# A Hymba block on one core: the MLP's first blocks by quarters of tokens, with their results kept in DRAM, and two orders between products

## The chip, the cores and the metric

The kernel runs on one core of a Trainium2 chip. The metric is the device time of one execution in microseconds (us). Three runs of the kernel before took 1572.6, 1574.49 and 1576.7 us; the median is 1574.49.

## The reference

One block of a streaming encoder, batch 1, 1024 tokens and 16 learned ones in front, width 1024, all float32. Cut to what matters here:

```python
h = concatenate([meta, x], axis=1)                      # 1040 tokens
h = h + token_mixer(rmsnorm(h, norm_mix_g), ...)        # ends with  mixed @ w_out
h = h + channel_mixer(rmsnorm(h, norm_ffn_g), ...)
return rmsnorm(h, norm_final_g)[:, N_META:]

def channel_mixer(u, w_up, w_gate, ffn_conv_w, w_down): # D_FF = 2816
    a = causal_dwconv(u @ w_up, ffn_conv_w)             # 3 taps along the tokens
    return (silu(a) * (u @ w_gate)) @ w_down
```

## The kernel before

Activations lie with features on the 128 partitions and tokens along the free axis. Every float32 matmul is made of three with a high and a low part of each operand (`mm3s`: high x high, low x high, high x low; lines L553, L554 and L555). ACT writes the high part of an operand (a cast, or a copy with a scale), DVE or POOL the low part (the difference).

Stages, in order of time: the mixer's projections and scans, head by head (to about 740 us); the output product with `w_out` (740 to 880); the second norm; the first block pair of the MLP; `xcomb`; the MLP's block pairs 1 to 10; the product with `w_down`; the last norm.

*Output product.* The class `Seven` makes a 2 x 2 block product from seven products instead of eight, in stages "1", "65", "73", "4" and "2"; `load`, `prep` (splits weights and sums of activations into parts) and `mms` (the matmuls) go step by step. Tokens are cut in two halves, A and B. Half B is complete after stage "73", so its norm runs beside stages "4" and "2"; half A is complete only at the end of stage "2", in two quarters of 256 tokens.

*Norm.* `rms` makes a column of sums of squares (`pcb`), takes root and reciprocal (`rcolb`), lets PE broadcast it along the partitions (`prb`), and ACT copies that to `Rb`. `scale_tasks` multiplies `resid` by `Rb` (L1026) and makes the high and low parts of the blocks `uh_g`/`ul_g` and `xh`/`xl` with the norm's gain (L967, L968).

*First block pair (pair 0).* `eight` makes it without sums of blocks: `pup` and `pga` are up and gate products, 24 matmuls each per output tile. `conv` applies the three taps on DVE (L1187, then two of L1189), silu on ACT (L1190) and the product with `Rb` (L1191, on DVE for pair 0, on POOL for the others); `gate` (L1223) multiplies with the gate product and writes the result to DRAM (`acts`), to be read by the last product.

*xcomb.* It makes the sums and differences of blocks that the products of seven need, for both quarters of a half (lines L964 to L993), eight calls of it.

*Pairs 1 to 10.* `seven(kind, i, ...)` with kind `up`, then `ga`: seven products into the PSUM banks x, y and z, in the order of `PROD`:

```python
PROD = (("x", 0, 0, 0), ("y", 0, 1, 1), ("x", 1, 0, 4), ("z", 1, 1, 3), ("x", 2, 0, 5), ("z", 2, 1, 2), ("x", 3, 0, 6))
```

Products 0 and 2 accumulate in x; ACT copies x out (`s2ga<-pga_x`, L1169) after product 2, and product 4 then goes on in the same bank. For `up` the tokens are in two chunks (258 and 256), for `ga` in one of 512. `need` loads and splits weights and runs its DVE steps (L261 to L266) and POOL steps (L243).

Which instruction comes first on an engine is decided when the program is built, by a list scheduler with planned times; code order and tile reuse bind it. `after(a, b)` binds one instruction to come behind another.

Of the kernel before, what the change touches and what calls it, by code (L numbers as in the profile page):

```python
# [17 lines left out]
P = 128  # L18
# [43 lines left out]
def body(ctx, tc, h_in, vecs, cst, mask_in, rot, w_v0, w_v, w_fm, w_out, w_up, w_gate, w_down, out):  # L62
# [234 lines left out]
    def rms(ss, t0, t1, nm, col, rb, ptags=("tr", "num"), eps=True):  # L297
# [14 lines left out]
        pr = rps("pr" + nm, ptags[1])  # L312
        for i, (o, w) in enumerate(subs):
            nc.tensor.matmul(pr[:, o:o + w], col[:w, i:i + 1].to_broadcast([w, P]), ident[:w, :w], start=True, stop=True)
        nc.scalar.copy(rb, pr[:, :n])
# [232 lines left out]
    def mm3s(pt, a, x, first, last):  # L548

        n = len(a)  # L550
        for k in range(n):
            (ah, al), (xh_, xl_) = a[k], x[k]
            nc.tensor.matmul(pt, ah, xh_, start=first and k == 0, stop=False, skip_group_check=True)  # L553
            nc.tensor.matmul(pt, ah, xl_, start=False, stop=False, skip_group_check=True)  # L554
            nc.tensor.matmul(pt, al, xh_, start=False, stop=last and k == n - 1, skip_group_check=True)  # L555
# [10 lines left out]
    class Seven:  # L566
# [3 lines left out]
        def __init__(self, nm, kn, wd, order, base, raw, rt, wlast, rlast, bank):  # L570
# [24 lines left out]

        def tsum(self, i, k):
# [3 lines left out]
        def prep(self, t):  # L600
# [5 lines left out]
            d = self.draws[t]  # L606
            act = self.act
            if st == self.order[-1]:
# [17 lines left out]
            else:  # L626
# [3 lines left out]
                self.ops[t] = [(half_of(w, 1), r7, "x"), (half_of(w, 0), r3, "y")]  # L630

# [73 lines left out]
    def wr(st, k, j):  # L705
        i = j + 2 * (k % 2) if st in ("65", "73") else k % 2 + 2 if st == "1" else k % 4
        if (st, k) == ("65", 0):
# [5 lines left out]
        return t[:, :HB], t[:, HB:2 * HB]  # L713

    def wbank(nm, b, j):
# [4 lines left out]
                 lambda k: tuple(wlate(x)[:, k * QT:(k + 1) * QT] for x in (0, 1)), wbank)  # L720
# [240 lines left out]
    def xput(i, k, j0, j1, src, g=None):  # L961
        hi, lo = (x[:, k, j0:j1] for x in xb(i))
        if g is None:
            nc.scalar.copy(hi, src)  # L964
            V.tensor_tensor(lo, src, hi.bitcast(F32), ALU.subtract)  # L965
        else:
            nc.scalar.activation(hi, src, AF.Copy, scale=g)  # L967
            V.scalar_tensor_tensor(lo, src, g, hi.bitcast(F32), ALU.mult, ALU.subtract)  # L968

    def xsingle(kb, t0, t1, half):  # L970
        g = vec[:, V_FFN + kb:V_FFN + kb + 1]
        i, o = ((kb // 4, TA), (2 if kb >= 4 else 6, TB))[half]
        xput(i, kb % 4, t0 - o, t1 - o, resid[:, kb, t0:t1], g)
# [4 lines left out]
    def xtile(nm, n):  # L978
        return fp2.tile([P, QT + 2], F32, tag="xc", name=nm, bufs=4)[:, :n]

    def xcomb(k, j0, j1):
# [5 lines left out]
        V.scalar_tensor_tensor(t3, B1, g1, u4, ALU.mult, ALU.subtract)  # L987
# [20 lines left out]
    def norm_tasks(t0, t1, mbs=range(KB), first=True):  # L1008
# [3 lines left out]
        def one(mb):  # L1012
            dst = ss if first and mb == mbs[0] else fp.tile([P, QT + 2], F32, tag="sqb", name=f"sqb{t0}_{mb}", bufs=2)[:, :n]
# [5 lines left out]
    def scale_tasks(t0, t1, tag):  # L1019
        def norm():  # L1020
            col = tmp.tile([P, 4], F32, tag="rcol", name=f"rcolb{t0}")
            rms(Rb[:, t0:t1], t0, t1, f"b{t0}", col, Rb[:, t0:t1], ptags=(tag, tag))

        def one(kb):
            x = resid[:, kb, t0:t1]
            V.tensor_tensor(x, x, Rb[:, t0:t1], ALU.mult)  # L1026
            xsingle(kb, t0, TA + XW if t1 == TB else t1, t0 >= TB)
# [15 lines left out]
    mixw.load(0)  # L1043
    mixw.load(2)
# [429 lines left out]
```

## Time and profile before

| | |
|---|---|
| median of three runs | 1574.49 us (1572.6 to 1576.7) |
| the profiled execution | 1575.96 us, span 1574.2 us |
| mean granted TensorE clock | 0.991 |
| busy: PE, DVE, ACT, POOL | 97%, 73%, 45%, 18% |
| one pair of the MLP's loop | 40.0 us |

The span is what the profiler recorded, from the first instruction to the last; the run's own time is 1.8 us longer. An engine's busy share is over the whole span. A row of the timeline gives start, duration, engine, line, operation and tiles, and in brackets how long the engine had been idle and what ended that. Lines are those of the kernel before.

### The profile page before, as it was taken

What the parts mean: (1) busy time and instruction counts of PE and PEld (TensorE: products, weight loads), DVE (VectorE), ACT (ScalarE), POOL (GpSimd) and SP (SyncE); (2) the same over time, 40 slices, a digit from 0 to 9 for tenths busy, and PEclk for the clock granted to TensorE, in tenths of its full rate; (3) what the DMA queues carried; (4) which work ended last, traced back from release to release, by engine and by line L of the source; (5) the groups of instructions that cost most, each with busy time, mean ns of one, the idle gap of its engine ahead of it and who ended that gap; (6) DMA issues with size and microseconds to landing.
All of it is one profiled execution on the core that took longest, in us unless ns stands there. A gap on an engine that the chain in (4) does not pass through costs nothing.

```text
span 1574.2 us, 25474 instructions
## 1 busy us (share of the span) xinstructions
PE 1524.2 (97%) x9701; PEld 1392.5 (88%) x9701; DVE 1146.2 (73%) x2342; ACT 714.1 (45%) x1468; POOL 277.3 (18%) x191
## 2 busy tenths in 40 slices
PE   7999999999999999999999899999999999999997
PEld 6999999999989999997888878888888888888876
DVE  8767768597858677679859787666676666777575
ACT  6574655545242535354347543333333334333363
POOL 0000000000000000000000005666666666000006
PEclk9999999999999999999999999999999999999999
DMA  6125445262625344245421111222222224832323
GB/s 211 41 69 170 153 119 181 81 217 88 213 80 176 115 147 144 88 130 197 175 90 58 48 38 72 79 81 80 75 81 81 81 81 150 331 111 90 103 65 108
DMA packets 86012, 184.83 MB, mean 117 GB/s; under 512 B 8249, under 2 KB 29441, under 8 KB 85889
## 3 DMA queue, kind: packets, MB, share of 16 engines
q1 hardware_dynamic: 85888, 183.20, 35.1%
q8 instruction: 76, 1.25, 0.3%
q14 instruction: 48, 0.39, 0.1%
HBM read 140.14 MB, written 43.03 MB: 116 GB/s over the span
## 4 chain that ended last, share of the span: by engine, by line
PE 79%; DVE 8%; DMA 7%; ACT 3%; issue 2%; POOL 1%; SPq 0%; DVEq 0%; ACTq 0%; POOLq 0%
PE pv L376 3%; PE pv L377 3%; PE pv L378 3%; PE po L388 3%; PE po L387 3%; PE po L386 3%; PE pga_x L553 2%; PE pup_x L553 2%; PE pup_x L555 2%; PE pup_x L554 2%; PE pga_x L555 2%; PE pga_x L554 2%; PE pdx L554 2%; PE pdx L555 2%; PE pdx L553 2%; PE pdy L553 2%
## 5 line engine op out<-in xcount | busy, mean ns | idle before, releaser
L1191 POOL TENSOR_TENSOR cv<-cv,Rb 128x512 f32<-128x512 f32 x40 | 62.9, 1573 | 993.4 <-ACT cv L1190 989.3
L376 PE MATMUL pv<-hi_v,uh 128*128 128x256 f32 (+1 forms) x512 | 146.6, 287 | 7.5 <-ACT hi_v L149 7.5
L378 PE MATMUL pv<-hi_v,ul 128*128 128x256 f32 (+1 forms) x512 | 145.1, 285 | 1.9 <-DVE ul L281 1.8
L377 PE MATMUL pv<-lo_v,uh 128*128 128x256 f32 (+1 forms) x512 | 145.6, 285 | 0.0
L386 PE MATMUL po<-uh,hi_o 128*128 128x386 f32 (+2 forms) x384 | 125.8, 328 | 0.0
L387 PE MATMUL po<-ul,hi_o 128*128 128x386 f32 (+2 forms) x384 | 123.8, 322 | 0.0
L388 PE MATMUL po<-uh,lo_o 128*128 128x386 f32 (+2 forms) x384 | 123.5, 322 | 0.0
L376 PEld LDWEIGHTS pv<-hi_v,uh 128*128 128x128 f32 x512 | 97.3, 190 | 10.1 <-ACT hi_v L149 7.5
L378 PEld LDWEIGHTS pv<-hi_v,ul 128*128 128x128 f32 x512 | 96.8, 190 | 2.4 <-DVE ul L281 2.3
L377 PEld LDWEIGHTS pv<-lo_v,uh 128*128 128x128 f32 x512 | 97.0, 189 | 1.0 <-DVE lo_v L150 0.9
L243 POOL TENSOR_TENSOR lo_ga<-fraw_ga,hi_ga 128x512 fp32r<-128x512 f32 (+1 forms) x50 | 87.1, 1749 | 40.4 <-ACT hi_ga L242 40.4
L243 POOL TENSOR_TENSOR lo_up<-raw_up,hi_up 128x512 fp32r<-128x512 f32 (+1 forms) x45 | 73.8, 1648 | 45.0 <-ACT hi_up L242 45.0
L242 ACT CAST hi_up<-raw_up 128x512 fp32r<-128x512 f32 (+1 forms) x52 | 36.4, 719 | 90.8 <-PE pga_z L554 46.9
L387 PEld LDWEIGHTS po<-ul,hi_o 128*128 128x128 f32 x384 | 72.9, 190 | 0.2
L386 PEld LDWEIGHTS po<-uh,hi_o 128*128 128x128 f32 x384 | 72.9, 190 | 0.1
L388 PEld LDWEIGHTS po<-uh,lo_o 128*128 128x128 f32 x384 | 72.7, 189 | 0.0
L554 PE MATMUL pup_x<-ul_g,hi_up 128*128 128x258 f32 (+1 forms) x240 | 67.1, 282 | 1.7 <-DVE ul_g L965 1.7
L242 ACT CAST hi_ga<-fraw_ga 128x512 fp32r<-128x512 f32 (+1 forms) x52 | 36.3, 717 | 70.1 <-PE pup_z L554 51.2
L553 PE MATMUL pup_x<-uh_g,hi_up 128*128 128x258 f32 (+1 forms) x240 | 67.1, 282 | 0.3 <-ACT s2up L1169 0.3
L555 PE MATMUL pup_x<-uh_g,lo_up 128*128 128x258 f32 (+1 forms) x240 | 66.1, 282 | 0.0
L386 PE MATMUL pq<-uh,hi_q 128*128 128x400 f32 (+2 forms) x192 | 63.1, 329 | 2.5 <-DVE vl L352 1.5
L386 PE MATMUL pk<-uh,hi_k 128*128 128x400 f32 (+2 forms) x192 | 62.4, 325 | 1.1 <-DVE kT L417 0.8
(701 smaller groups left out, 5166.4 us busy)
## 6 DMA issues: line engine op xcount, KB each, us to landing
wsd<-w_down_d SPq DMA_DIRECT2D x22, 512.0 KB, 4.2
wsd<-wsd SPq DMA_DIRECT2D x44, 256.0 KB, 2.1
raw_up<-w_up_d SPq DMA_DIRECT2D x22, 512.0 KB, 3.5
fraw_ga<-w_gate_d SPq DMA_DIRECT2D x22, 512.0 KB, 3.7
acts<-cv SPq DMA_DIRECT2D x44, 256.0 KB, 2.0
rd<-wsd SPq DMA_DIRECT2D x22, 512.0 KB, 3.4
wsw<-w_out_d SPq DMA_DIRECT2D x16, 512.0 KB, 4.2
raw_o<-w_fm_d SPq DMA_DIRECT2D x16, 512.0 KB, 3.5
```

The lines of the kernel that those rows point to most:

```text
L242: nc.scalar.copy(hi[:, o:o + n], x)
L243: (eng or nc.gpsimd).tensor_tensor(lo[:, o:o + n], x, hi[:, o:o + n].bitcast(F32), ALU.subtract)
L376: nc.tensor.matmul(pv[:L, :nv], a, hi[:, o:o + nv], start=kb == 0, stop=False)
L377: nc.tensor.matmul(pv[:L, :nv], a, lo[:, o:o + nv], start=False, stop=False)
L378: nc.tensor.matmul(pv[:L, :nv], b, hi[:, o:o + nv], start=False, stop=kb == KB - 1)
L386: nc.tensor.matmul(pt[:, :n], a, uh[kb][:, t0:t1], start=kb == 0, stop=False)
L387: nc.tensor.matmul(pt[:, :n], a, ul[kb][:, t0:t1], start=False, stop=False)
L388: nc.tensor.matmul(pt[:, :n], b, uh[kb][:, t0:t1], start=False, stop=kb == KB - 1)
L553: nc.tensor.matmul(pt, ah, xh_, start=first and k == 0, stop=False, skip_group_check=True)
L554: nc.tensor.matmul(pt, ah, xl_, start=False, stop=False, skip_group_check=True)
L555: nc.tensor.matmul(pt, al, xh_, start=False, stop=last and k == n - 1, skip_group_check=True)
L1191: (G if i else V).tensor_tensor(cv, cv, Rb[:, t0 + 2:t0 + XW], ALU.mult)
```

## The change

1. Pair 0's conv, silu, product with `Rb` and gate product leave the passage between norm and loop. `first_up` and `first_gate` copy the up and gate products out of PSUM and write them to DRAM (`kept`, eight writes). `gate_part(i)` for i = 1 to 4 calls `first_out`, which reads one (m, half) back and does `conv` and `gate` on it. The product with `Rb` is on POOL for all pairs.
2. The products of pair 0 for half A are cut by quarters of tokens: up (0 to 256, 256 to 514) and gate (2 to 256, 256 to 514), in the order up first quarter, gate first quarter, up second quarter, `xcomb` of the first quarter, gate second quarter, `xcomb` of the second.
3. Half B's norm is done in one piece of 514 tokens instead of 258 and 256.
4. Two orders: in `seven` the first product in z (n = 3) starts after product 2 has ended (`ends[2]`), and the first DVE operation of every `xcomb` but the first comes after the last scaled operand (`last["scaled"]`).
5. The output product's stage-4 weights are split during stages "65"/"73" into tiles of their own (`pre4`, `wfour`); weight loads go out four ahead of the reads (`pump`), and the tiles of stage 2's split weights are shared by halves.
6. The chunks of `up` are 256 and 258 wide; `xcomb`'s scratch tiles are shared in pairs with those that `first_out` reads into (`spare_out`).

The diff, cut to that:

```diff
+            if n == 3 and ci == 0:
+                after(m[0], ends[2])
+            ends[n] = m[1]
...
-        (G if i else V).tensor_tensor(cv, cv, Rb[:, t0 + 2:t0 + XW], ALU.mult)
+        nc.gpsimd.tensor_tensor(cv, cv, Rb[:, t0 + 2:t0 + XW], ALU.mult)
...
+    kept = {(kind, m, half): dram.tile([P, n], F32, name=f"kept_{kind}{m}{half}") for kind, n in (("up", XW), ("ga", HB)) for m in range(2) for half in range(2)}
+    UC = [(0, QT), (QT, XW)]
...
-            nc.scalar.copy(c0[m, half][:, slice(*chunks[ci])], pt)
-        eight("up", half, chunks, bank, done)
+            nc.scalar.copy(c0[m, half][:, slice(*UC[ci])], pt)
+            if ci:
+                nc.sync.dma_start(kept["up", m, half], c0[m, half][:, :XW])
+        eight("up", half, *UC[ci], lambda m: pp(f"pup0_{m}{half}{ci}", tags[m]), done)
...
+        def done(m, pt):
+            if j1 == XW:
+                x = ftile(f"g0_{m}{half}")
+                nc.scalar.copy(x[:, :HB], gbank[m, half])
+                nc.sync.dma_start(kept["ga", m, half], x[:, :HB])
+        eight("ga", half, j0, j1, bank, done)
...
-    def convs(half):
-        for m in range(2):
-            conv(0, m, half, c0[m, half])
-
-    first_up(1, lambda nm, m: pp(nm))
-    g = first_gate(1, lambda nm, m: pp(nm))
-    convs(1)
-    g()
-    first_up(0, lambda nm, m: fps(nm, "xy"[m]))
-    for k in range(4):
-        xcomb(k, 0, QT)
-    g = first_gate(0, lambda nm, m: fps(nm, "y"))
-    convs(0)
-    g()
-    for k in range(4):
-        xcomb(k, QT, XW)
-
-    UC = [(0, 258), (258, XW)]
+    def first_out(m, half):
+        c, g = (spare_out(f"{x}0b_{m}{half}") for x in "cg")
+        nc.sync.dma_start(c[:, :XW], kept["up", m, half])
+        nc.sync.dma_start(g[:, :HB], kept["ga", m, half])
+        conv(0, m, half, c)
+        gate(0, m, half, g[:, :HB])
+
+    for ci in range(2):
+        first_up(1, ci, ("pp", "pp"))
+    first_gate(1, 2, XW, ("pp", "pp"))
+    first_up(0, 0, ("pp", "sA"))
+    first_gate(0, 2, QT, ("sA", "num"))
+    first_up(0, 1, ("pp", "tr"))
+    for k in range(4):
+        xcomb(k, 0, QT)
+    first_gate(0, QT, XW, None)
+    for k in range(4):
+        xcomb(k, QT, XW)
...
         seven("ga", i, [(2, XW)], done)
+        if i < 5:
+            first_out((i - 1) % 2, (i - 1) // 2)
...
-    BQ, AQ = [(MB, MB + QT + 2), (MB + QT + 2, T)], [(MA, MA + QT), (MA + QT, MB)]
+    BQ, AQ = [(MB, T)], [(MA, MA + QT), (MA + QT, MB)]
...
+        if k or j0:
+            after(x, last["scaled"])
...
+            if mixw.steps[u][0] == "73" and u % 2 and u + 7 not in mixw.four:
+                mixw.pre4(u + 7)
```

ACT in the passage, where the second quarter of half A is normed, before (`sqb`: squares, `rcolb`: the root, `cv_11`: pair 0's conv result, `xu`, `xt`, `xv`: scratch of `xcomb`):

```order
L310 ACTIVATE rcolb_10438<-pcb_10439,epsc 128x2
L967 ACTIVATE uh_g<-xu_0_10836,vec 128x256
L964 CAST uh_g<-xv_0_10838 128x256
L986 ACTIVATE xu_0_10852<-resid,vec 128x256
L1190 ACT_TABLE_LOAD
L1190 ACTIVATE cv_11_10704<-cv_11_10704 128x512
L315 COPY Rb<-prb_10444 128x256
L964 CAST uh_g<-xt_0_10853 128x256
L967 ACTIVATE uh_g<-xu_0_10852,vec 128x256
L967 ACTIVATE uh_g<-resid,vec 128x258 x4
```

The same place in the changed kernel (`c`, `g`: copies of pair 0's products):

```order
L310 ACTIVATE rcolb_10389<-pcb_10390,epsc 128x2
L1270 COPY c_01_10514<-pup_011_10543 128x258
L1013 ACTIVATE xh_10205<-resid,vec 128x256
L1010 CAST uh_g<-xv_0_10824 128x256
L1013 ACTIVATE uh_g<-xu_0_10823,vec 128x256
L1270 COPY c_11_10541<-pup_111_10570 128x258
L1284 COPY g_01_10634<-pga_01_10609 128x512
L319 COPY Rb<-prb_10395 128x256
L1013 ACTIVATE uh_g<-resid,vec 128x258 x4
```

Between the root and the copy of `Rb` the table load and the silu are gone, and copies of products stand there.

PE at the same place, before: `prb` and the products that come next.

```order
L555 MATMUL pup_100_10741<-xh_10248,lo_up_1_10243 128x256
L304 MATMUL pcb_10439<-cs,Rb 128x1 x2
L314 MATMUL prb_10444<-cs,rcolb_10438 128x128 x2
L553 MATMUL pup_101_10794<-uh_g,hi_up_1_10242 128x258
L553 MATMUL pga_000_10884<-uh_g,hi_ga_0_10526 128x512
```

Now (`pup_100`, 24 matmuls, and the first quarter of `pga_00`, 24 matmuls, follow `prb`; `pup_101`, the first that reads the second quarter, stands 49 rows behind it, and `pcb` 50 rows ahead):

```order
L560 MATMUL pga_01_10609<-xh_9830,lo_ga_0_10486 128x512
L316 MATMUL prb_10395<-cs,rcolb_10389 128x128 x2
L558 MATMUL pup_100_10692<-uh_g,hi_up_1_10199 128x256
L559 MATMUL pup_100_10692<-ul_g,hi_up_1_10199 128x256
L560 MATMUL pup_100_10692<-uh_g,lo_up_1_10200 128x256
```

Before, `pcb` and `prb` followed the same up product, and the second quarter was read right behind them.

ACT in the loop around `s2ga`, in pair 2, before:

```order
L1190 ACTIVATE cv_01_11598<-cv_01_11598 128x512
L1169 COPY s0ga_11671<-pga_x_11658 128x512
L1190 ACTIVATE cv_10_11645<-cv_10_11645 128x512
L242 CAST hi_ga_3_11689<-fraw_ga_1_11380 128x512
L1169 COPY s2ga_11705<-pga_x_11658 128x512
L242 CAST hi_up_0_11722<-raw_up_0_11604 128x1024
```

and now, with the silu of the deferred piece (`cv_10_11779`):

```order
L1247 ACTIVATE cv_01_11589<-cv_01_11589 128x512
L1226 COPY s0ga_11662<-pga_x_11649 128x512
L242 CAST hi_ga_3_11680<-fraw_ga_1_11359 128x512
L1247 ACTIVATE cv_10_11636<-cv_10_11636 128x512
L1247 ACTIVATE cv_10_11779<-cv_10_11779 128x512
L1226 COPY s2ga_11696<-pga_x_11649 128x512
```

The cast of `hi_ga_3` has moved ahead of the silu of `cv_10`, and the deferred piece's silu stands between that and `s2ga`. DVE there, now (`c0b`: read back from DRAM):

```order
L261 TENSOR_TENSOR s_6_11751<-raw_up_1_11597 128x512
L1244 TENSOR_SCALAR cv_10_11636<-c_10_11633,vec 128x512
L1244 TENSOR_SCALAR cv_10_11779<-c0b_11775,vec 128x512
L262 TENSOR_TENSOR raw_up_1_11597<-raw_up_1_11597,raw_up_0_11595 128x512
L1246 SCALAR_TENSOR_TENSOR cv_10_11636<-c_10_11633,vec,cv_10_11636 128x512
L1246 SCALAR_TENSOR_TENSOR cv_10_11779<-c0b_11775,vec,cv_10_11779 128x512
L1246 SCALAR_TENSOR_TENSOR cv_10_11636<-c_10_11633,vec,cv_10_11636 128x512
L1246 SCALAR_TENSOR_TENSOR cv_10_11779<-c0b_11775,vec,cv_10_11779 128x512
```

Every second operation is the deferred piece's; before, `cv_10`'s three stood there alone. On PE, the gate product of a pair was y, ten matmuls of z's first product, x's product 2 (twelve), two of z and x's product 4; it is y, twelve of x, twelve of z, and product 4.

More of the change, by code (lines that the diff above doesn't have):

```diff
@@ L1012, in one @@
         def one(mb):
[L1013 removed]
+            dst = ss if first and mb == mbs[0] else (ftile(f"sqb{t0}_{mb}") if n > HB else fp.tile([P, QT], F32, tag="sqb", name=f"sqb{t0}_{mb}", bufs=2))[:, :n]
             nc.scalar.activation(dst, resid[:, mb, t0:t1], AF.Square)
@@ L1079, in body @@
             break
-        for u in range(t, t + 5):
-            mixw.load(u)
+        if t == 0:
+            mixw.pump()
         if st == "65" and k == 1:
@@ L1118, in body @@
     for k in range(KW):
-        for u in range(T2 + k, T2 + k + 5):
-            mixw.load(u)
         mixw.prep(T2 + k + 1)
@@ L1150, in seven @@
         banks = {}
+        ends = {}
         j00 = chunks[0][0]
```

124 lines of the change are left out of this document (83 added, 41 removed).

## The prediction

> **What bounds the kernel now.** I read the page first, then the table of stretches, then the waits of PE, and last the timeline of the stretches where PE waits. Ahead of everything stands one fact of the page: PE is the engine that counts.
>
> ```profile
> span 1574.2 us, 25474 instructions
> PE 1524.2 (97%) x9701; PEld 1392.5 (88%) x9701; DVE 1146.2 (73%) x2342; ACT 714.1 (45%) x1468; POOL 277.3 (18%) x191
> ```
>
> Only 50 us of the span are idle on PE, and the change keeps the number of products, so it can win only PE's idle time and time at a low clock. It touches two places: the passage from the output product to the MLP (850 to 951 us) and the MLP's loop. The stretches (span, then PE, PEld, DVE, ACT, POOL, clock, DMA share, GB/s) show where these lose:
>
> ```profile
> 900.00:905.00 5.00, 1.02 (x6) 0.66 (x4) 3.79 (x11) 4.06 (x9) 0.00 (x0) 0.59 0.00 0
> 905.00:910.00 5.00, 3.14 (x11) 2.51 (x11) 5.00 (x15) 2.12 (x7) 0.00 (x0) 0.50 0.00 0
> 940.00:945.00 5.00, 2.62 (x18) 2.02 (x16) 5.00 (x13) 2.39 (x6) 0.00 (x0) 1.00 0.42 129
> 1000.00:1040.00 40.00, 39.80 (x254) 35.74 (x253) 27.50 (x34) 14.03 (x27) 25.87 (x17) 1.00 0.26 80
> ```
>
> The loop has little to give: PE is busy 39.80 us of 40. The passage has two holes, around 900 and 941. Of PE's waits the longest of the passage (850 to 980) and the only one of the loop (965 to 1345) are (us in total, times, longest):
>
> ```profile
> PE pup L553 <- ACT uh_g L967: 4.0, 1, 4.0
> ```
>
> ```profile
> PE pga_x L553 <- ACT s2ga L1169: 2.6, 10, 0.8
> ```
>
> **Part 1: the three stalls of the passage, as they are priced now.** The timeline of PE:
>
> ```profile
> 857.14 0.40 PE L553 MATMUL pup<-xh,hi_up 128*128 128x256 f32 x2
> 858.66 0.38 PE L554 MATMUL pup<-xl,hi_up 128*128 128x256 f32 x1 [1.12 <-DVE xl L968]
> ...
> 899.64 0.71 PE L314 MATMUL prb<-cs,rcolb 128*128 128x128 f32 x4 [1.10 <-DVE rcolb L311]
> 904.33 0.58 PE L553 MATMUL pup<-uh_g,hi_up 128*128 128x258 f32 x1 [3.98 <-ACT uh_g L967]
> 907.20 0.58 PE L554 MATMUL pup<-ul_g,hi_up 128*128 128x258 f32 x1 [1.86 <-DVE ul_g L968]
> ...
> 911.20 0.29 PE L554 MATMUL pup<-ul_g,hi_up 128*128 128x258 f32 x1
> ...
> 943.58 0.39 PE L554 MATMUL pup_x<-ul_g,hi_up 128*128 128x258 f32 x1 [1.70 <-DVE ul_g L965]
> ...
> 945.37 0.58 PE L553 MATMUL pup_z<-uh_g,hi_up 128*128 128x258 f32 x1 [1.05 <-DVE cv L1223]
> ...
> 948.74 0.28 PE L553 MATMUL pup_z<-uh_g,hi_up 128*128 128x256 f32 x1
> ```
>
> - Stall 0 (half B's low parts, `xl`): the two matmuls from 857.14 take 0.40 us where one alone takes 0.28 (948.74), so matmuls of this width follow each other every 0.12 us and the next could start at 857.38; it starts at 858.66: 1.3 us.
> - Stall 1 (second quarter of half A): idle 1.10 + 3.98 + 1.86 = 6.9 us. From there matmuls run at half clock until 911.20 (the stretch 905 to 910 shows 0.50): from 904.33, 6.9 us less the 1.86 idle, 5.0 us at half speed, 2.5 lost. Together 9.4 us.
> - Stall 2 (the sums `xcomb` for the first block pair of seven products): idle 1.70 + 1.05 us, and half clock from 945.37 to 948.74, of which half, 1.7, is lost. Together 4.5 us.
>
> Why stall 1 is there is in the rows of ACT and DVE at that moment:
>
> ```profile
> 899.95 1.28 ACT L1190 ACT_TABLE_LOAD   x1
> 901.25 0.63 ACT L1190 ACTIVATE cv<-cv 128x512 f32<-128x512 f32 x1
> 901.78 0.36 ACT L315 COPY Rb<-prb 128x256 f32<-128x256 f32 x1
> ...
> 903.37 0.51 ACT L967 ACTIVATE uh_g<-xu,vec 128x256 fp32r<-128x256 f32 x1 [0.93 <-DVE xu L990]
> ...
> 901.91 0.69 DVE L1191 TENSOR_TENSOR cv<-cv,Rb 128x512 f32<-128x512 f32 x1 [1.21 <-ACT cv L1190]
> ...
> 903.25 2.77 DVE L1026 TENSOR_TENSOR resid<-resid,Rb 128x256 f32<-128x256 f32 x8
> ...
> 906.27 0.48 DVE L968 SCALAR_TENSOR_TENSOR ul_g<-xu,vec,uh_g 128x256 fp32r<-128x256 f32 x1
> ```
>
> The scale row `Rb`, for which `prb` was just made, is copied by ACT only behind a table load and a silu of block pair 0; DVE then stands on a `cv` operation and scales the quarter only at 903.25.
>
> **What the change does to them.** In the new order no conv, silu, Rb or gate operation of pair 0 lies in the passage. What leaves DVE there is in the view of one tile, `cv`, from 870 to 946:
>
> ```profile
> L1189 DVE SCALAR_TENSOR_TENSOR cv<-c,vec,cv x8: 744/746/749, 877.9 to 938.6; 128x512 f32<-128x512 f32 x8
> L1187 DVE TENSOR_SCALAR cv<-c,vec x4: 479/480/482, 877.1 to 931.6; 128x512 f32<-128x512 f32 x4
> L1191 DVE TENSOR_TENSOR cv<-cv,Rb x4: 679/688/693, 881.4 to 942.5; 128x512 f32<-128x512 f32 x4
> L1223 DVE TENSOR_TENSOR cv<-pga,cv x4: 678/684/691, 896.7 to 945.2; 128x512 f32<-128x512 f32 x4
> ```
>
> 8 x 0.746 + 4 x (0.480 + 0.688 + 0.684) = 13.4 us; as back-to-back operations overlap by some 0.08 us, about 11.7 of DVE's time.
> - Stall 0: half B's norm in one 514-wide piece puts its first products behind the whole of stage 2 (some 6 us later on PE), where its `xl` has been written. Gain 1.3 us. Bounds: 0 if the 514-wide square sums make the norm end just as much later, 1.3 at the best.
> - Stall 1: the copy of `Rb` loses the silu in front of it, `prb` goes ahead of a whole up-product of 24 matmuls, and 24 matmuls of the gate product's first half (254 wide) are put between that and the first one that needs the second quarter. That is 48 x 0.12 = 5.8 us of cover, against a chain from `prb` (Rb copy 0.36, eight scalings 2.77, then a scale by ACT like the one at 903.37, 0.51, and a low part by DVE like the one at 906.27, 0.48) of 4.1 us. All 9.4 us go; bounds 4.7 (the DVE chain is again held up by something in front) and 9.4.
> - Stall 2: PE reaches the sums about 1.3 + 9.4 = 10.7 us earlier. DVE has 11.7 us less, but not all of it lies ahead of the sum that PE waits for: of the four gate operations two lie at 944.63 or later, and in the new order DVE waits some 2 us for a cast by ACT. I walked the new DVE order from the second quarter's scaling on (50 operations of the sums at about 0.39 us, 6.7 us of others between them) and come out 0 to 4 us behind PE. I take 2 us of idle time and, since 1.70 + 1.05 us of idle cost a halved clock, another 1.5: 3.5 left of 4.5, a gain of 1.0. Bounds: loss 1.5, gain 4.5.
> - The split gate product has 96 matmuls of half the width for 48 of 512: two of 0.12 us against one of some 0.235 (two starts below, 1011.56 and 1011.79, lie 0.23 apart), so 0.2 us more.
> - The stage-4 operands split ahead, the halved stage-2 tiles and earlier loads (`pump`) lie in stretches where PE doesn't wait: nothing, bounds -0.5 and +1.
>
> The Trainium skill ("TensorE: Matmul & The Clock Gate", the Part 1 on the HAM clock gate) says that the clock is halved after an idle window of about 3.4 us and restored after about 3.4 us of work. The 3.37 us at half clock from 945.37 agree with the second number; the first doesn't, since the idle pieces there were 1.70 and 1.05 us. By the rule my residual stall of 2 us would cost only itself, and the sum would be 1.5 us better.
>
> Passage: -1.3 - 9.4 - 1.0 + 0.2 = -11.5 us.
>
> **Part 2: the loop.** The timeline of one iteration, PE first, then ACT, DVE and POOL of the iteration after:
>
> ```profile
> 1010.62 0.40 PE L555 MATMUL pga_z<-uh_g,lo_ga 128*128 128x512 f32 x1
> 1011.22 0.50 PE L553 MATMUL pga_x<-uh_g,hi_ga 128*128 128x512 f32 x1 [0.20 <-ACT s2ga L1169]
> 1011.56 0.39 PE L554 MATMUL pga_x<-ul_g,hi_ga 128*128 128x512 f32 x1
> 1011.79 0.40 PE L555 MATMUL pga_x<-uh_g,lo_ga 128*128 128x512 f32 x1
> ...
> 1049.20 0.63 ACT L1190 ACTIVATE cv<-cv 128x512 f32<-128x512 f32 x1 [5.18 <-DVE cv L1189]
> 1049.74 0.60 ACT L242 CAST hi_ga<-fraw_ga 128x512 fp32r<-128x512 f32 x1
> 1050.60 0.59 ACT L1169 COPY s2ga<-pga_x 128x512 f32<-128x512 f32 x1 [0.26 <-PE pga_x L555]
> ...
> 1042.80 1.78 DVE L261 TENSOR_TENSOR s<-raw_up 128x512 f32<-128x512 f32 x1
> 1044.50 1.52 DVE L1187 TENSOR_SCALAR cv<-c,vec 128x512 f32<-128x512 f32 x1
> 1045.94 1.78 DVE L262 TENSOR_TENSOR raw_up<-raw_up,raw_up 128x512 f32<-128x512 f32 x1
> ...
> 1045.70 1.47 POOL L1191 TENSOR_TENSOR cv<-cv,Rb 128x512 f32<-128x512 f32 x1
> 1049.91 1.73 POOL L1191 TENSOR_TENSOR cv<-cv,Rb 128x512 f32<-128x512 f32 x1 [2.74 <-ACT cv L1190]
> ```
>
> Bank x is wanted again when ACT has copied it (`s2ga`). PE's gap is 1011.22 - 1010.62 - 0.23 = 0.37 us, and the restart, 0.34 to the next instead of 0.23, makes it 0.48. With `after`, the x product ends 10 x 0.23 = 2.3 us sooner and twelve z matmuls (2.8 us) cover the copy. But the copy stays behind silu and cast on ACT: it could start at 1049.74 + 0.60 = 1050.34 instead of 1050.60. So 0.3 us are won per iteration, at most 0.48: six iterations (5 to 10) give -1.8.
>
> In iterations 1 to 4 a deferred piece of pair 0 is worked in: DVE gets a TENSOR_SCALAR and two SCALAR_TENSOR_TENSOR between those of `cv_10`, ACT a silu ahead of `s2ga`, POOL one more product with Rb, DVE a gate product. DVE is full from 1042.80 on. The added TENSOR_SCALAR meets POOL at work until 1045.70 + 1.47 = 1047.17, so it costs about 1.5 like the one at 1044.50; `L262` then runs after POOL and is 1.1 shorter (0.69 like L1191's above, for 1.78). The first added SCALAR_TENSOR_TENSOR costs 0.66 (0.746 less the overlap), so `cv_10` is ready about 1.5 - 1.1 + 0.66 = 1.0 later. Behind it come two silus of 0.55 and the copy (0.59); the cast goes ahead. From 1049.20 + 1.0, the copy ends near 1051.9; PE would go on at 1050.8 (0.37 before the copy's present end, 1050.60 + 0.59): a stall of 1.0 instead of 0.48, so +0.5 each, +2.0. Bounds per iteration: -0.5 and +2.5.
>
> Loop: -1.8 + 2.0 = +0.2 us (bounds -4.7 and +10).
>
> **Sum.** -11.5 + 0.2 = -11.3 us. The profiled execution took 1575.96 us (span 1574.2), so 1564.7 by its own time. It stands 1.5 us above the median of the runs, 1574.49; against that the sum gives 1563.2, the forecast. The range of the terms: -9.4 - 1.3 - 4.5 - 4.7 with the split's 0.2 gives 1554.8; the poor ends together (stall 1 at 4.7, stall 2 at +1.5, loop +5 at half its bound) 1576.
>
> **The rivals.**
> - *More is won*: stall 2 vanishes, too, and the loop wins 0.4 each time: -9.4 - 1.3 - 4.5 + 0.2 - 4 = -19 us, 1555.5. For it: DVE loses 11.7 us of work and ACT two table loads of 1.28. Against: DVE is at 5.00 of 5 around 941. Chance 0.15.
> - *DVE becomes the bound of the passage*: the second quarter or the sums come only half as much earlier, since the products with Rb were never what filled DVE: stall 1 gives 4.7, stall 2 loses 1.5: -1.3 - 4.7 + 1.5 + 0.2 = -4.3, with the loop 1570.4. Chance 0.13.
> - *Slower: the deferred conv runs into POOL.* Where POOL is busy, DVE's TENSOR_TENSOR takes 1.78 us (1042.80) and its TENSOR_SCALAR 1.52 (1044.50). If POOL, with one more product of 1.5 us per iteration, works on beyond 1047.17, the three added DVE operations cost 1.5 + 1.7 + 1.7 (the 1.78 less the overlap), `cv_10`'s own two 1.0 more each, and the added silu 0.55: 7.5 us on `s2ga`, 7 on PE, 28 in four iterations: -11.5 - 1.8 + 28 = +14.7, 1589. It decides from 13.3 / 4 = 3.3 us of added wait per iteration on. Against it: POOL sits idle for 2.74 us before 1049.91 and is busy only 25.87 us of 40. Chance 0.09. The Trainium skill ("GPSIMD Engine Reference", Specifications) states that POOL's SBUF interface is shared with VectorE's instructions that read two SBUF inputs or run in a 2-port mode, which speaks against moving this work next to POOL; the rows at 1042.80 and 1044.50 agree.
> - *Nothing moves*: half B's norm in one piece holds up the first products by as much as the rest wins: 1574. Chance 0.06.
>
> **How the numbers follow.** My forecast, 1558 to 1568, has 0.57. About 0.3% (4.7 us) is what a measurement of this kernel can tell from no change, so faster means below 1569.8. Forecast and first rival are faster, of the second some half: 0.79. Same: the other half and most of the last, 0.11. Slower: 0.10. The range takes in the second rival and most of the first: 1553 to 1572.
>
> **Signs.** Right: PE's waits for `uh_g`, `ul_g` in `pup` are gone, and the clock is 1.00 between 885 and 905; the first pair's `pup_x` begins some 11 us earlier; ACT's copy of `Rb` follows no table load; what is left of idle time is in front of pair 1's products, 1 to 3 us; `pga_x` waits for `s2ga` near 0.5 to 1 us in four iterations and 0.2 or less in six. Wrong: a new wait of PE in stage 2 or at the first `pup`, DVE operations of 1.5 us between `cv_10` and `s2ga` right up to the silu, or iterations 1 to 4 over 41 us.

## The result and the profile after

| | before | changed |
|---|---|---|
| median of twelve runs each | 1574.41 us (1571.8 to 1579.1) | 1576.64 us (1572.2 to 1581.8) |
| ratio | | 1.0012, 95% interval 0.9998 to 1.0026 |
| the profiled execution (span) | 1575.96 us (1574.2) | 1575.30 us (1573.2) |

No change that can be measured, where 11 us less were forecast; 1576.64 lies above the forecast's range of 1553 to 1572. The page of the changed kernel, its first line and the line of engines:

```profile
span 1573.2 us, 25559 instructions
PE 1528.0 (97%) x9749; PEld 1398.2 (89%) x9749; DVE 1157.6 (74%) x2318; ACT 711.4 (45%) x1457; POOL 283.1 (18%) x195
```

The two profiled executions already differ ahead of the changed passage. One product of the output product that stands alike in both starts 3.20 us earlier in the second. Over all kernels of this document its start varies from 739.3 to 745.2 us, so this says nothing of the change, and everything below is counted from it (before, then changed; timeline of PE):

```profile
743.66 0.47 PE L553 MATMUL pwy<-wtq,hi_w 128*128 128x512 f32 x1 [0.79 <-DVE mm L854]
```

```profile
740.46 0.47 PE L558 MATMUL pwy<-wtq,hi_w 128*128 128x512 f32 x1 [0.79 <-DVE mm L900]
```

The views of the tiles `pup_x` and `pga_y` (ns min/median/max, first and last start) give the first product of pair 1 and its first gate product in y, before and then changed:

```profile
L553 PE MATMUL pup_x<-uh_g,hi_up x240: 276/282/387, 934.1 to 1314.0; 128*128 128x258 f32 x70, 128*128 128x256 f32 x50
L553 PE MATMUL pga_y<-xh,hi_ga x40: 391/394/397, 962.4 to 1324.9; 128*128 128x512 f32 x40
```

```profile
L558 PE MATMUL pup_x<-uh_g,hi_up x240: 275/282/582, 919.9 to 1312.5; 128*128 128x256 f32 x69, 128*128 128x258 f32 x51
...
L558 PE MATMUL pga_y<-xh,hi_ga x40: 391/394/397, 949.9 to 1323.5; 128*128 128x512 f32 x40
```

So the execution splits into four pieces (us; the third ends with the loop's last matmul of `pga_x`):

| piece | before | changed | difference | forecast |
|---|---|---|---|---|
| mark to first `pup_x` (stalls 0 and 1, the split) | 190.4 | 179.5 | -10.9 | -10.5 |
| first `pup_x` to first `pga_y` (stall 2) | 28.4 | 30.0 | +1.6 | -1.0 |
| first `pga_y` to the loop's end | 378.7 | 389.7 | +11.0 | +0.2 |
| from there to the end | 233.1 | 233.6 | +0.5 | 0 |

They sum to +2.2, like the difference of the medians; such close agreement is luck, as single executions of one kernel spread over 7 to 10 us. Ahead of the first `pup_x` the gain came as forecast, and the loop took it back. PE's waits from 700 to 990 in the changed kernel, and below them those of the loop (965 to 1345):

```profile
PE pga_x L558 <- ACT s2ga L1226: 2.7, 1, 2.7
PE pup_x L559 <- DVE ul_g L1011: 1.0, 1, 1.0
PE pup_z L559 <- DVE ul_g L1014: 0.8, 1, 0.8
...
PE pup_x L558 <- ACT uh_g L1010: 0.6, 1, 0.6
```

```profile
PE pga_x L558 <- ACT s2ga L1226: 6.7, 4, 2.0
```

The waits of `pup` for `uh_g`, `ul_g` and `xl` (4.0, 1.9 and 1.1) are gone. What was 0.2 us in each pair is 2.7 and three times 2.0. The stretches show it by place: full clock where stall 1 was, a stall 2 as large as ever at 930, and four iterations of 42 to 44 us before they come down to 39.7:

```profile
900.00:905.00 5.00, 5.00 (x42) 4.91 (x42) 2.97 (x5) 2.10 (x2) 0.00 (x0) 1.00 0.12 10
...
930.00:935.00 5.00, 2.50 (x9) 1.45 (x7) 4.40 (x9) 3.51 (x7) 1.27 (x1) 0.89 0.00 0
935.00:940.00 5.00, 5.00 (x22) 4.61 (x22) 2.61 (x7) 2.00 (x6) 0.00 (x0) 0.50 0.37 105
```

```profile
949.93:994.10 44.17, 41.44 (x254) 37.03 (x252) 34.37 (x38) 14.98 (x28) 28.32 (x19) 0.96 0.27 90
994.10:1037.45 43.35, 41.40 (x253) 36.91 (x252) 33.54 (x38) 14.98 (x28) 27.49 (x18) 0.96 0.26 92
1037.45:1079.35 41.90, 39.91 (x254) 35.85 (x253) 33.19 (x38) 14.98 (x28) 27.61 (x18) 1.00 0.29 95
1079.35:1122.75 43.40, 41.45 (x253) 36.96 (x252) 33.56 (x38) 14.99 (x28) 27.52 (x18) 0.96 0.23 79
1122.75:1162.45 39.70, 39.70 (x253) 35.80 (x252) 27.56 (x34) 14.35 (x27) 26.09 (x17) 1.00 0.23 80
```

No engine but PE is anywhere near full in these iterations: DVE 34.4 of 44, POOL 28. It is one chain at one place. The timeline there, PE, then DVE, POOL and ACT:

```profile
958.09 0.39 PE L560 MATMUL pga_z<-uh_g,lo_ga 128*128 128x512 f32 x1
961.20 0.80 PE L558 MATMUL pga_x<-uh_g,hi_ga 128*128 128x512 f32 x1 [2.73 <-ACT s2ga L1226]
...
952.73 1.51 DVE L1244 TENSOR_SCALAR cv<-c,vec 128x512 f32<-128x512 f32 x1
954.16 1.51 DVE L1244 TENSOR_SCALAR cv<-c0b,vec 128x512 f32<-128x512 f32 x1
955.59 1.78 DVE L262 TENSOR_TENSOR raw_up<-raw_up,raw_up 128x512 f32<-128x512 f32 x1
957.28 0.74 DVE L1246 SCALAR_TENSOR_TENSOR cv<-c,vec,cv 128x512 f32<-128x512 f32 x1
957.95 0.74 DVE L1246 SCALAR_TENSOR_TENSOR cv<-c0b,vec,cv 128x512 f32<-128x512 f32 x1
958.61 0.74 DVE L1246 SCALAR_TENSOR_TENSOR cv<-c,vec,cv 128x512 f32<-128x512 f32 x1
...
955.33 1.48 POOL L243 TENSOR_TENSOR lo_ga<-fraw_ga,hi_ga 128x512 fp32r<-128x512 f32 x1
...
959.38 1.29 ACT L1247 ACTIVATE cv<-cv 128x512 f32<-128x512 f32 x2 [6.02 <-DVE cv L1246]
960.58 0.57 ACT L1226 COPY s2ga<-pga_x 128x512 f32<-128x512 f32 x1
```

The order is the one shown ahead of the prediction. The surprise is `L262`: 1.78 us, not 0.69, while POOL works on `lo_ga` beside it (955.33 to 956.81). That is the low part of `hi_ga_3`, whose cast moved ahead of the silus on ACT; e8 below tests that it is the cause.

### The profile page after: what moved, and what is told of

It is laid out like the page before. It is cut to its first block, busy times and chain, and to the rows that moved or that the text cites. A ratio compares the mean times of both kernels' runs of the same rounds, so it can differ in the third digit from the quotient of the medians.

```text
span 1573.2 us, 25559 instructions
## 1 busy us (share of the span) xinstructions
PE 1528.0 (97%) x9749; PEld 1398.2 (89%) x9749; DVE 1157.6 (74%) x2318; ACT 711.4 (45%) x1457; POOL 283.1 (18%) x195
## 4 chain that ended last, share of the span: by engine, by line
PE 79%; DVE 8%; DMA 7%; ACT 3%; issue 2%; POOL 1%; SPq 0%; DVEq 0%; ACTq 0%; POOLq 0%
PE pv L380 3%; PE pv L381 3%; PE pv L382 3%; PE pga_x L558 2%; PE pup_x L559 2%; PE po L391 2%; PE po L392 2%; PE po L390 2%; PE pup_x L558 2%; PE pup_x L560 2%; PE pga_x L559 2%; PE pga_x L560 2%; PE pdx L559 2%; PE pdx L560 2%; PE pdx L558 2%
## 5 line engine op out<-in xcount | busy, mean ns | idle before, releaser
L1248 POOL TENSOR_TENSOR cv<-cv,Rb 128x512 f32<-128x512 f32 x44 | 67.6, 1541 | 980.3 <-ACT cv L1247 967.9
L559 PE MATMUL pup_x<-ul_g,hi_up 128*128 128x256 f32 (+1 forms) x240 | 68.2, 286 | 1.0 <-DVE ul_g L1011 1.0
L558 PE MATMUL pup_x<-uh_g,hi_up 128*128 128x256 f32 (+1 forms) x240 | 68.0, 285 | 0.6 <-ACT uh_g L1010 0.6
L560 PE MATMUL pup_x<-uh_g,lo_up 128*128 128x256 f32 (+1 forms) x240 | 66.7, 284 | 0.0
```

What stands on the lines that cost most here:

```text
L558: m.append(nc.tensor.matmul(pt, ah, xh_, start=first and k == 0, stop=False, skip_group_check=True))
L560: m.append(nc.tensor.matmul(pt, al, xh_, start=False, stop=last and k == n - 1, skip_group_check=True))
L1248: nc.gpsimd.tensor_tensor(cv, cv, Rb[:, t0 + 2:t0 + XW], ALU.mult)
```

## The experiments

All are compared with the kernel before, run on the same chip; the rows come from several chips, so rows are compared by their ratios. The pieces are those of the table above, each read from one execution's timeline (mark to first `pup_x`; mark to first `pga_y`; the loop). The changed kernel, e1, e2 and e8 have the same instructions up to `pga_y` but for small swaps, and differ there by up to 1.6 us: a smaller difference in the first two pieces shows nothing.

| kernel | median, us | ratio (95%) | to `pup_x` | to `pga_y` | loop |
|---|---|---|---|---|---|
| before | | 1 | 190.4 | 218.8 | 378.7 |
| changed | 1576.64 | 1.0012 (0.9998 to 1.0026) | 179.5 | 209.5 | 389.7 |
| e1, silu behind | 1571.11 | 0.9965 (0.9952 to 0.9977) | 179.5 | 209.5 | 384.0 |
| e2, conv and silu behind | 1564.13 | 0.9924 (0.9911 to 0.9938) | 178.0 | 207.9 | 377.6 |
| e3, no deferred work | 1563.69 | 0.9922 (0.9909 to 0.9935) | 181.1 | 211.3 | 376.4 |
| e8, cast behind (one run) | 1571.95 | | 177.9 | 207.9 | 383.8 |
| e4, z order alone | 1576.38 | 0.9997 (0.9984 to 1.0010) | 191.8 | 220.8 | 375.6 |
| e5, conv back in the passage | 1568.74 | 0.9958 (0.9943 to 0.9974) | 179.0 | 212.6 | 377.4 |
| e9, e2 with whole gate product | 1563.93 | 0.9924 (0.9903 to 0.9946) | 178.5 | 205.7 | 378.4 |
| e12, e5 with whole gate product | 1571.27 | 0.9973 (0.9958 to 0.9988) | 181.2 | 214.6 | 377.1 |
| e15, e2 with norm in two pieces | 1565.98 | 0.9937 (0.9916 to 0.9958) | 180.2 | 209.2 | 378.2 |
| e16, e12 with norm in two pieces | 1572.09 | 0.9977 (0.9959 to 0.9996) | 182.9 | 216.7 | 376.9 |
| e17, order of sums alone | 1571.37 | 0.9982 (0.9967 to 0.9997) | 188.3 | 216.7 | 378.6 |
| e7, e2, pair 1's conv and silu behind | 1566.55 | 0.9941 (0.9923 to 0.9959) | 179.5 | 204.1 | 383.2 |
| e10, e2, pair 1's silu behind | 1560.73 | 0.9901 (0.9886 to 0.9916) | 178.0 | 205.4 | 378.5 |
| e11, e2, table load early | 1566.79 | 0.9938 (0.9922 to 0.9953) | 181.0 | 209.7 | 378.6 |

### Where the loop lost it: e1, e2, e3, e8

In `conv`, cut to the orders (`x` is its first DVE operation, `y` its silu); e2 has both, e1 the second alone:

```diff
+        if i == 0:
+            after(x, last["conv"])      # DVE: behind cv_10's last operation
...
+        if i == 0:
+            after(y, last["s2"])        # ACT: behind the copy s2ga
```

> The changed kernel, with one more order on ACT: the silu of the deferred piece of pair 0 (iterations 1 to 4) stands behind the copy s2ga, not ahead of it. DVE, POOL and PE keep their order. Theory A (the stall before x's product 4 in iterations 1 to 4 is DVE's chain: the added operations between those of cv_10 make cv_10 late by 2 to 3 us, the added silu only adds 0.6): PE still waits for s2ga in all four iterations, 0.6 us less each, 2.1 us in the first and 1.4 in the others; first to last gate product of the loop 3 to 7 us shorter, the upper end if no half clock follows. Rival B (the added silu is what holds the copy): no wait left in the four iterations and the loop 14 us shorter, about 1562 us.

> The changed kernel, with two more orders in iterations 1 to 4: the deferred piece's first DVE operation stands behind the last conv operation of cv_10, and its silu behind the copy s2ga. The same work is done. Theory A (order on DVE and ACT is the whole of the loss): cv_10's silu comes at the same place of the iteration as in iterations 5 to 10, PE's wait for s2ga falls from 1.95 to 2.73 us to under 0.3 in all four, periods 39.7 instead of 41.9 to 44.2, 14 us less, about 1562 us. Rival C (DVE, POOL or the queue of loads have no room for the deferred work in these iterations, wherever it stands): PE waits elsewhere in them, periods stay over 41, less than 6 us gained.

With the silu behind (e1), the waits are 2.13, 1.29, 1.36 and 1.29 us, 0.6 to 0.7 less each, and the loop is 5.7 us shorter: theory A's size, and rival B falls. In three iterations the clock stays up, too (41.16 to 41.28 us). With the conv's DVE operations behind as well (e2), PE waits for `s2ga` twice in the whole loop, in the first pair (0.68) and the last (0.77); e2's waits of PE from 885 to 1345:

```profile
PE pga_x L558 <- ACT s2ga L1226: 1.4, 2, 0.8
PE pup_x L559 <- DVE ul_g L1011: 1.0, 1, 1.0
PE pup_z L559 <- DVE ul_g L1014: 0.8, 1, 0.8
PE pup_x L558 <- ACT uh_g L1010: 0.5, 1, 0.5
```

The same work is done in the same iterations, and the loop is 12.1 us shorter. Rival C falls: DVE, POOL and the queue have the room.

```diff
-        if i < 5:
-            first_out((i - 1) % 2, (i - 1) // 2)
-                nc.sync.dma_start(kept["ga", m, half], x[:, :HB])
+                nc.sync.dma_start(acts[m, half], x[:, :HB])
```

> The changed kernel without the deferred work: pair 0's conv, silu, product with Rb and gate product are left out, and the gate product alone is written to DRAM in their place. This prices the deferred work in the loop. Theory A: periods 39.7 in all iterations, passage as in the changed kernel, 14 us less than it, within 1 us of the run with both orders. Rival C: clearly below that run. Rival D (the loss is not in the deferred work, but in the clock after the long stall of the passage): periods of 42 and more stay.

e3 has the time of e2 (0.9922 and 0.9924) and periods of 39.7 but for a first one of 40.3. In the two profiles the loop is 1.2 us shorter without the deferred work; once in order, that work is free to within what these runs can tell, and rival D falls.

```diff
+        # fstep, the last piece of the gate weights, pairs 1 to 4
+        after(last["cast"], last["silu"])    # ACT: cast of hi_ga_3 behind cv_10's silu
```

> The changed kernel with one order on ACT in pairs 1 to 4: the cast of the gate weights' last piece (hi_ga_3) stands behind the silu of cv_10 again, as in the kernel before; deferred work where it is in the changed kernel. It asks why DVE's L262 still took 1.78 us where the forecast had 0.69. If it is POOL's low part of that weight, which the earlier cast lets run beside L262: L262 0.7 to 0.8 us in pairs 1 to 4, the silu of cv_10 1.1 us earlier against y's first product, PE's waits for s2ga 1.95 less 1.1, plus the cast's 0.5 which now stands between, so 1.4. If POOL's product with Rb alone does it: L262 stays over 1.5 and the waits grow by 0.5.

The timeline of e8 (a single run) at the same place, DVE, POOL, ACT:

```profile
956.83 1.51 DVE L1247 TENSOR_SCALAR cv<-c0b,vec 128x512 f32<-128x512 f32 x1
958.26 0.68 DVE L262 TENSOR_TENSOR raw_up<-raw_up,raw_up 128x512 f32<-128x512 f32 x1
...
962.90 1.73 POOL L243 TENSOR_TENSOR lo_ga<-fraw_ga,hi_ga 128x512 fp32r<-128x512 f32 x1
...
960.96 0.63 ACT L1250 ACTIVATE cv<-cv 128x512 f32<-128x512 f32 x1 [6.06 <-DVE cv L1249]
```

`L262` takes 0.68 us in each of the four pairs, where it took 1.78 in all four, as `lo_ga` now starts 4.6 us behind it. POOL's product with `Rb` is there in both, so `lo_ga` is the cause. The silu of `cv_10` comes 960.96 - 952.57 = 8.4 us behind y's first product, where it was 959.38 - 949.93 = 9.45: 1.06 us, as foretold. The waits are 2.05, 1.23, 1.27 and 1.23.

### The order between products: e4

```diff
+                if n == 3 and ci == 0:
+                    after(m[0], ends[2])
+                ends[n] = m[1]
```

> The kernel before, with one part of the change alone: the first product in z starts behind the end of product 2, in all pairs. Expected by the loop of the changed kernel (iterations 5 to 10 took 39.70 to 39.79 us where they took 40.02 to 40.10): 0.3 us in each of ten iterations, 3.3 us less than before, 1571 us, and no wait of PE for s2ga but in the last pair. If the gain needs the earlier cast of hi_ga_3 or another part of the change, nothing.

In the profile the loop is 3.1 us shorter with periods of 39.66 to 39.75, as expected. The twelve runs show nothing (0.9984 to 1.0010, against 0.9979 expected); in the profiled one the passage, where the order of instructions is the same but for details of pair 1, was 2.0 us longer. Part of an answer may lie in the clock: the granted clock of the twelve runs is 0.9888 in the mean, against 0.9897 in the seventeen of the kernel before. Over 1575 us that would be 1.4 us lost (an estimate, from clocks given to three places; so few runs don't make the difference sure). Why the runs don't show the loop's gain stays open.

### What took stall 1 away: e5, e9, e12, e15, e16, e17

> The changed kernel with the deferral alone undone: pair 0's conv, silu, product with Rb (on DVE) and gate product stand in the passage again, straight from the copies and from PSUM; the quarters, half B's norm in one piece and both orders stay. If the deferral is what shortened the passage, the first gate product of pair 1 comes 5 to 9 us later than in the changed kernel (counted from the same product of the output product), PE waits again for the second quarter; with the loop at 376 us instead of 390 the sum is 1567 to 1572. If quarters and norm alone do it, the passage stays and the time is 1562.

> The run with both orders, with the gate product of pair 0's half A in one piece of 512 again, made behind both quarters of the up product. It prices the quarters as cover: 24 matmuls less (2.9 us) between the row of scales (prb) and the first product that reads the second quarter. By the forecast's chain of 4.1 us from prb against 24 x 0.12 = 2.9 us of cover, PE waits 1.2 us or more there, up to 3, and another 1.7 if the clock halves: 1 to 4.5 us more than with both orders. If the chain is shorter than forecast: no wait, the same time.

> The run with pair 0's conv and gate back in the passage, and with the gate product of half A in one piece as well (two parts of the change undone). It tells whether either of the two covers alone takes stall 1 away: with deferral and whole gate PE waited 0.5 us there, with conv back and quarters not at all. If they are redundant covers, then with both gone stall 1 returns: PE waits 2 us or more for the second quarter, up to 9 with the half clock, 3 to 9 us more than with conv back alone. If the norm of half B in one piece (and the earlier row of scales) is what took it away: no wait over 1 us and the same time as with conv back.

> The run with both orders, with half B's norm in two pieces (258 and 256) again. In this order the row of scales of the second quarter (prb) stands 24 + 3 matmuls later on PE than with one piece, so that only 21 matmuls cover the chain behind it. If the one piece is what brought the row of scales forward: PE waits 1.5 to 3 us in front of the second quarter's products, with up to 3 us of half clock, and stall 0 (1.1 us, xl) is back: 3 to 6 us more than with both orders. If it doesn't matter: within 1 us.

```diff
 e5   in first_gate's done, instead of the copy and the write to kept:
+                conv(0, m, half, c0[m, half])
+                gate(0, m, half, gbank[m, half])
...          (and first_out is no longer called)
 e9   (on e2), e12 (on e5):
-    first_gate(0, 2, QT, ("sA", "num"))
...
-    first_gate(0, QT, XW, None)
+    first_gate(0, 2, XW, ("sA", "num"))
 e15  (on e2):
+    BQ, AQ = [(MB, MB + QT + 2), (MB + QT + 2, T)], [(MA, MA + QT), (MA + QT, MB)]
...          (and half B's norm tasks for both pieces)
```

I took the deferral for the cause of stall 1's end. With conv back (e5), PE reaches the first `pup_x` as early as in the changed kernel (179.0). Table load and first silu are again ahead of the copy of `Rb`, but done before `prb` came: the copy waited 0.62 us for `prb`. What the deferral does is further on: e5 pays it at stall 2, where its longest wait of PE (850 to 985) is the first row here. Its first gate product of pair 1 comes 3.1 us later than in the changed kernel, not the 5 to 9 expected; its whole time lies 0.0036 of before, 5.7 us, over e3's. e9 shows that the quarters bring nothing that can be measured once conv is away. Idle time of PE in front of the second quarter was 0 in e5, 0.5 in e9, 0.9 in e15 and 1.7 in e12 (second row), against 6.9 before:

```profile
PE pup_z L558 <- ACT uh_g L1013: 4.8, 1, 4.8
```

```profile
PE pup L559 <- DVE ul_g L1014: 1.7, 1, 1.7
```

> The run with conv back and whole gate product, and half B's norm in two pieces as well: three parts of the change undone, the orders, quarter-wise copies and early operands stay. With only two of them undone PE waited 1.7 us in front of the second quarter at most. In this order prb stands right in front of the second quarter's products again, as in the kernel before. If each of the three parts was enough by itself against stall 1 (redundant covers): stall 1 is back in full, PE waits 5 to 7 us there and runs at half clock for some 5, pair 1's first product 8 to 11 us later than in the run with conv back and whole gate, 1576 to 1582. If one of the parts that stay took it away: waits under 2 us there, 1569 to 1574.

> The kernel before, with one part of the change alone: the order that puts the sums (xcomb, but for the first) behind the last scaled operand. On DVE the second quarter's eight scalings move nine rows up, past operations of the sums that came to some 4 us; conv, silu and table load stay ahead of the copy of Rb. If this order is the part that was still at work when three others were undone: stall 1's idle 6.9 us falls to 2 to 4 and the half clock goes, pair 1's first product 4 to 7 us earlier than in the kernel before, 1569 to 1573. If ACT's table load and silu ahead of Rb set the stall: idle time stays at 6 us or more and the time within 2 us of before.

```diff
 e16 = e12 and e15's line;  e17 = the kernel before and:
+        if k or j0:
+            after(x, last["scaled"])     # sums behind the last scaled operand, on DVE
```

With three parts undone (e16), 1.5 + 1.6 us of idle time came back, at full clock, between the two outcomes expected. With the order of the sums alone on the kernel before (e17), the idle 6.9 us became 0.55 + 2.63 + 1.19 = 4.4, but the half clock did not go: it lasted from 900.72 to 909.08, longer than before (904.33 to 911.20), and PE came to `pup_x` 2.1 us earlier, not the 4 to 7 expected. The timelines of e16 and of e17 at that place (0.39 and 0.58 us are the same matmul at full and at half clock):

```profile
898.87 0.39 PE L558 MATMUL pup<-uh_g,hi_up 128*128 128x258 f32 x1 [1.47 <-ACT uh_g L1013]
901.07 0.39 PE L559 MATMUL pup<-ul_g,hi_up 128*128 128x258 f32 x1 [1.58 <-DVE ul_g L1014]
```

```profile
897.37 0.71 PE L314 MATMUL prb<-cs,rcolb 128*128 128x128 f32 x4 [0.55 <-DVE rcolb L311]
900.72 0.58 PE L553 MATMUL pup<-uh_g,hi_up 128*128 128x258 f32 x1 [2.63 <-ACT uh_g L967]
902.92 0.58 PE L554 MATMUL pup<-ul_g,hi_up 128*128 128x258 f32 x1 [1.19 <-DVE ul_g L968]
...
897.14 1.28 ACT L1192 ACT_TABLE_LOAD   x1
898.43 0.63 ACT L1192 ACTIVATE cv<-cv 128x512 f32<-128x512 f32 x1
898.97 0.35 ACT L315 COPY Rb<-prb 128x256 f32<-128x256 f32 x1
```

So the stall had no one cause: the order of the sums takes some 2.5 us of its idle time by itself. Deferral, quarters and norm are covers of which any one can be missing at no more than 0.9 us of idle time. In e17 the table load and silu are still ahead of `Rb`; in e16 they were done before `prb`. What beside the order of the sums keeps e16 at full clock and its idle time 1.3 us shorter than e17's, no run separates: the early operands, the earlier loads and the shared tiles (parts 5 and 6 of the change) and what is left of the quarters (part 2) were not run alone.

### The stall that is left in the passage: e7, e10, e11

> The run with both orders (deferred conv and silu behind), and pair 1's first conv and its silu (with the table load of 1.28 us) put behind the last sum of blocks, on DVE and on ACT. It asks whether the stall left in the passage (PE waits of 0.80, 0.54 and 0.95 us, then 6.7 us at half clock) is the same pattern as stall 1 was: a table load and a silu ahead of small casts. If so: the waits fall below 0.5 in sum, no half clock, 3 to 5.5 us less than with both orders, about 1560. If DVE has too many sums for PE in any case: 1 us or less.

> The run with both orders, and only the silu of pair 1's first conv (with its table load) put behind the last cast of the sums on ACT; that conv's DVE operations stay among the sums. It takes the half of the former run that can't meet POOL. If the table load and silu (1.28 + 0.55 us on ACT ahead of two casts) make the wait of DVE of 0.56 and PE's of 0.54 and 0.95 us: these fall by about 1 us in sum, and if the clock is not halved any more another 3 us; first interval of the loop as with both orders (40.8). 1 to 4 us less than with both orders. If DVE's own order sets the end of the sums: the same time.

> The run with both orders, and a silu of one column behind the last root of the norm of half A, so that the table load comes there and not ahead of pair 1's first silu. The load alone (1.28 us) leaves the place at 930. Expected: 0.5 to 1 us less waiting there, 3 more if the clock stays up; a loss of up to 1.3 if the load now holds up ACT between root and copy of Rb. Between 4 less and 1 more than with both orders.

```diff
 e7   pair 1's first conv:
+        if (i, m, half) == (1, 0, 0):
+            after(x, last["xd"])            # DVE: behind the last sum (e7 alone)
...
+        if (i, m, half) == (1, 0, 0):
+            after(y, last["xa"])            # ACT: behind the last sum's cast (e7, e10)
 e11  behind the last root of half A's norm:
+    after(nc.scalar.activation(warm, epsc, AF.Silu), last["sqrt"])
```

In e2 the table load had only moved: it stood at 930.17, ahead of the casts of the last sums. e7 shortens the way to `pga_y` by 3.8 us against e2 and loses 5.6 in the loop, where the first interval is 46.45 us: the conv put back runs beside POOL (one operation of 0.74 us took 2.26), and PE waits 1.8 us for `s0ga` and 1.8 for the cast `hi_up`; that POOL is the cause was not tested. e10, with the silu alone behind, keeps 2.5 of it and loses 0.9. It is the fastest kernel here, 0.9901 (0.9886 to 0.9916) of before; its interval overlaps e2's a little (0.9911 to 0.9916), so that it beats e2 is likely, not shown. e11 was not faster than e2: 0.9938, with the way to `pup_x` 3 us longer in its profile. The expected gain is refuted; whether it lost is not settled, as the intervals overlap.

## Why the prediction was right or wrong

- **Stalls 0 and 1 (right, for a reason that was too narrow).** -10.5 with the split foretold, -10.9 measured; that they agree to 0.4 us is luck, as the same instructions took 1.6 us less in e2 and e8. I credited the missing silu and table load and 48 matmuls of cover. e5 and e9 show that each could be missing; e17, that the order of the sums, which I had not priced at all, did part of it: in the timeline of before, DVE works on two sums at 902.52 and 902.91, between the copy of `Rb` and the scaling. Stall 0, which I credited to the norm in one piece, is also gone in e15 and e16, which have two.
- **Stall 2 (wrong size).** Foretold 3.5 us left of 4.5. Left were 0.15 + 0.80 + 0.55 + 0.96 = 2.5 us idle and half clock from 933.87 to 940.56, 3.3 lost: 5.8 (timeline of the changed kernel, the first and the last ones at half clock and the next):

```profile
933.87 0.58 PE L559 MATMUL pup_x<-ul_g,hi_up 128*128 128x258 f32 x1 [0.96 <-DVE ul_g L1011]
...
940.34 0.42 PE L560 MATMUL pup_x<-uh_g,lo_up 128*128 128x258 f32 x1
...
940.76 0.28 PE L559 MATMUL pup_x<-ul_g,hi_up 128*128 128x258 f32 x1
```

  The idle time was near the 2 foretold. The half clock lasted twice as long as the 3.4 us I took from the old stall; why, no run shows. The Trainium skill's figure ("TensorE: Matmul & The Clock Gate", Part 1) of about 3.4 us until the clock is restored agrees with the loop (1005.6 to 1009.0 at half clock), not with this place.
- **Loop, iterations 5 to 10 (right).** -0.3 each foretold, 40.02 to 40.10 became 39.69 to 39.79.
- **Loop, iterations 1 to 4 (the step that failed).** I forecast +0.5 each, +2.0; it was +12.7 (172.82 us for four periods that took 160.16). The failed sentence is "`L262` then runs after POOL and is 1.1 shorter". I had the order of ACT on the page, with the cast of `hi_ga_3` ahead, and used it for ACT only. That cast also releases POOL's low part, so POOL was not idle where the trace of before showed it idle. Hence the silu of `cv_10` came 1.9 us late behind y's first product (in the second iteration 1002.76 - 994.10 = 8.66, before 1049.20 - 1042.48 = 6.72), not 1.0; in the first iteration, 2.7. e8 puts the price of this at 1.06 us. Iterations over 41 us, a sign of being wrong that I had named, came. The loop's +11.0 lies even above the bound of +10; by its own terms the lower bound would be -4.9, not -4.7, which decides nothing.
- **The clock, which the loop term left out.** Idle pieces of 2.73 and 1.95 us cost about 1.6 us more each by half clock, in three of four iterations. I had just counted that for stall 2. Idle time grew from 0.8 to 8.6 us; the rest of the 12.7, 4.9, is about three times 1.6.
- **The rival "the deferred conv runs into POOL"** had the place and the mechanism, at 0.09, but its price of 7 us per iteration was twice too high and its point of decision (3.3 us) about what came: 3.2 us. What met DVE was not the added product with `Rb` that it named, but the low part; only `L262` was slower than forecast, and the added SCALAR_TENSOR_TENSOR took 0.74 us, not 1.7. My argument against it, POOL's 2.74 us of idle time, was a row of the kernel before, where the cast came later.

The changed kernel's parts did what they were for. Two orders of one line each (e2) turn no change into 12 us less.

## What to carry to other kernels

Work that is moved next to a critical copy must be placed on every engine it uses: one added silu and three added DVE operations in front of a 0.6 us copy cost 3.2 us an iteration here, with the half clock that the waits brought, and nothing that could be measured behind it. When an order moves one cast forward, ask what the cast releases on the next engine and what runs beside that; an idle stretch in the old trace is no evidence once its releaser has moved. Look where a table load goes when its place is cleared: here it went ahead of the next casts.

## What the runs showed of the hardware

- Idle pieces under 2 us were followed by half clock, but not each time. The second iteration's timeline:

```profile
1004.58 0.50 PE L558 MATMUL pga_x<-uh_g,hi_ga 128*128 128x512 f32 x1 [1.95 <-ACT s2ga L1226]
...
1005.64 0.63 PE L559 MATMUL pga_x<-ul_g,hi_ga 128*128 128x512 f32 x1
...
1009.03 0.28 PE L558 MATMUL pup_x<-uh_g,hi_up 128*128 128x256 f32 x1
```

  After 1.95 us PE ran at half clock from about 1 us after the restart for 3.4 us (1005.6 to 1009.0; again in the fourth iteration, 1090.9 to 1094.2), after 1.99 us not at all (1037.45 to 1079.35 has 1.00), and in e1 after 1.29 to 1.36 us in none of three. The Trainium skill's window of about 3.4 us of idleness ("TensorE: Matmul & The Clock Gate", Part 1) would not have cut it after any of these. Its statement that this window runs free would fit that one of three like cases was spared; no run here shows the window's phase.
- One POOL operation on two tiles in SBUF beside it made a DVE TENSOR_TENSOR of 0.68 us take 1.78 (e8 against the changed kernel, the same instruction). The Trainium skill ("GPSIMD Engine Reference", Specifications) states the shared interface; its price here is 1.1 us an operation.
